# Twenty-six columns of an input projection by Strassen's seven products, ahead of a paged decode

## Chip, cores and metric

One NeuronCore of a Trainium2 chip runs the whole kernel. The metric is the device time of one execution in microseconds, lower is better. The kernel before has a median of 1408.3 us over three runs (1408.06 to 1410.06).

## What is computed

One layer of an inference step over 512 prompt tokens and 32 decode tokens (8 sequences of 4). Everything is float32.

```python
h = rmsnorm(x, norm_w)
p = jnp.einsum('btd,de->bte', h, w_in)          # 2048 x 8192
qa, ka, va, za, qb, fb, ib, zb = jnp.split(p, offs, axis=-1)   # 8 heads of 128 each
# group A: stick-breaking attention; the decode tokens also read 2048 past tokens from a paged cache
z = jnp.einsum('bqhd,bkhd->bhqk', q, k) * scale + bias
log_1m = jnp.where(causal, jax.nn.log_sigmoid(-z), 0.0)
tail = lax.cumsum(log_1m, axis=3, reverse=True) - log_1m
w = jnp.where(causal, jnp.exp(jax.nn.log_sigmoid(z) + tail), 0.0)
o_a = jnp.einsum('bhqk,bkhd->bqhd', w, v)
# group B: HGRN2 recurrence, exact per token, in chunks
S_t = diag(f_t) S_{t-1} + k_t v_t^T;  o_t = S_t^T q_t
m = concat(head_rmsnorm(o_a) * silu(za), head_rmsnorm(o_b) * silu(zb))
y = rmsnorm(x + m @ w_out, final_norm_w)
```

The keys, the values and the recurrent states of the new tokens are outputs too.

## The kernel before

The 544 tokens are kept normalised and transposed in SBUF as `h_hi` and `h_lo`, two float32r parts whose sum is the token value, in two halves of the 2048 inputs (`kh`). The input projection has 64 column tiles of 128 columns; `project` (L381) computes one of them in PSUM as 96 matmuls: two halves of the inputs, two halves of the tokens (256 and 288 of them, `HALVES`), eight slices of 128 inputs, and three part products each (weight hi by token hi, weight hi by token lo, weight lo by token hi). L408 scales the result on its way to SBUF. The weights come 512 KB at a time: `load_ahead` (L244) issues the transfer on SP's queue into `wraw` (three buffers), `split_ahead` (L252) makes `whi` on ACT (L259) and `wlo` on DVE (L260), and `weights_piece` (L268) keeps both ahead of the matmuls. The output projection (L1106) takes its weights in the same way.

The order on PE and SP is written by a small planner, `Flow`. It walks over the matmuls of the projection, and every two groups of four it may put in a piece of a side job. A side job is a generator that yields its cost, a time it should wait, and a gate: the share of the columns that must be done before. The other engines' instructions are put in an order that fits this one. The columns are taken in this order: the 8 q columns of group A, kept in DRAM (`q_dram`, L957); then in `group_a` (L927) k, v and z_a of each head, with its `attend` (L455) as a side job; then in `group_b` (L1007) q_b, f, i and z_b of each head, with its `hgrn` (L705). Next to both runs `decode` (L645): 32 key steps (L678) of 1/32 of the cached keys each, whose pages SP fetches (`k_fetch`, L540, 2 MB a step, three `kpage` buffers of 1 MB) and DVE transposes (L550), and 32 value steps (L688), 4 steps behind, on pages of `v_fetch` (L561, 2 MB a step, ten `vpage` buffers of 256 KB). The 36 steps are spread evenly by their gate between 1/8 and 0.87 of the columns:

```python
yield (32 * 56.0 if keys else 0.0) + (8 * 213.0 if values else 0.0), \
    (8000.0 if step == 0 else 3000.0), 0.0, start + (stop - start) * step / NSTEP
```

In `hgrn`, SP loads the head's old states into two `bst` tiles (L724), `usp` (L897) and L900 on DVE update them at the end of the head, and L902 on POOL stores them. A head is begun when the one before has issued these stores (`hg_done`). After the last column come the rest of the output projection and the final norm.

## Time and profile before

| | |
|---|---|
| median of three runs | 1408.3 us |
| the profiled execution, its own time | 1405.46 us |
| its span in the trace | 1403.8 us |
| PE busy | 1331.7 us (95%) |
| DVE, ACT, POOL busy | 758.3, 413.6, 311.7 us |
| projection matmuls (L401) | 6144 |
| HBM read and written | 239.15 and 19.53 MB |
| granted TensorE clock | 0.985 of full speed |

The profiled execution took 1.66 us more than its span, and the median lies 2.8 us above it. Busy times are averages over stages with different limits: the first columns run alone on PE, then the columns share it with decode, and behind them come the last columns and the output projection. Each stage has to be read for itself.

### The profile page before, as it was taken

The numbers are of one execution on the slowest core, as the hardware profiler recorded it, in microseconds if no ns is written. First come the engines' busy times: TensorE is split into PE (matmuls) and PEld (weight loads), VectorE is DVE, ScalarE is ACT, GpSimd is POOL, SyncE is SP. The second block draws the span as 40 slices with busy tenths as digits, with TensorE's granted clock in tenths as the row PEclk, the third lists the DMA queues.
The fourth block names the chain that finished last, engine by engine and source line by source line (L and its number), as shares of the span: only waits on it lengthen the run. The fifth ranks groups of instructions, "written<-read, shape, count | busy, mean of one in ns | idle before, by whom it ended". The sixth has DMA issues, their size and how long they took to land.

```text
span 1403.8 us, 30662 instructions
## 1 busy us (share of the span) xinstructions
PE 1331.7 (95%) x11922; PEld 1215.2 (87%) x11922; DVE 758.3 (54%) x1302; ACT 413.6 (29%) x701; POOL 311.7 (22%) x577
## 2 busy tenths in 40 slices
PE   6999999899999999999989989999999999999997
PEld 6999888798988888888887978889899897988996
DVE  6324555647466474667575674665455658222223
ACT  6211324224233242331222231132323225222223
POOL 3212113112132121132332232121213324111001
PEclk9999999999999999999999999999999999999999
DMA  7338876699989898898888978746523251622223
GB/s 218 109 109 214 200 203 163 174 292 235 280 228 269 236 258 220 229 273 212 247 231 233 274 193 235 229 143 196 149 61 113 65 194 42 240 76 78 89 76 143
DMA packets 245027, 260.69 MB, mean 186 GB/s; under 512 B 13497, under 2 KB 169842, under 8 KB 244178
## 3 DMA queue, kind: packets, MB, share of 16 engines
q1 hardware_dynamic: 237600, 235.00, 60.5%
q0 software_dynamic: 5504, 15.80, 3.3%
q10 hardware_dynamic: 1778, 7.93, 1.5%
q8 instruction: 94, 1.54, 0.5%
q14 instruction: 51, 0.42, 0.1%
HBM read 239.15 MB, written 19.53 MB: 184 GB/s over the span
## 4 chain that ended last, share of the span: by engine, by line
PE 74%; issue 10%; DVE 9%; DMA 3%; ACT 3%; POOL 1%; SPq 0%; DVEq 0%; POOLq 0%; ACTq 0%
PE pacc L401 42%; PE yacc L1106 13%; DVE kpage L550 3%; PE av L688 3%; PE dzp L678 3%; PE sp L746 2%; DMA kpage<-in_cache_k 2%; PE op L507 1%; PE usp L897 1%; PE ysp L1115 1%; DVE wlo L260 1%; DMA wraw<-in_w_in 1%; DVE lt L450 1%; DVE att L803 1%; PE wp L174 1%
## 5 line engine op out<-in xcount | busy, mean ns | idle before, releaser
L401 PE MATMUL pacc<-h_hi,whi 128*128 128x256 f32 (+1 forms) x2048 | 546.4, 299 | 15.2 <-ACT whi L259 9.8
L401 PE MATMUL pacc<-h_lo,whi 128*128 128x256 f32 (+1 forms) x2048 | 530.4, 289 | 0.0
L401 PEld LDWEIGHTS pacc<-h_hi,whi 128*128 128x128 f32 x2048 | 389.1, 190 | 40.1 <-issue 22.9
L401 PEld LDWEIGHTS pacc<-h_lo,whi 128*128 128x128 f32 x2048 | 389.2, 190 | 1.7 <-issue 0.2
L260 DVE TENSOR_TENSOR wlo<-wraw,whi 128x1024 fp32r<-128x1024 f32 x160 | 198.0, 1240 | 199.0 <-PE yacc L1106 78.0
L259 ACT CAST whi<-wraw 128x1024 fp32r<-128x1024 f32 x160 | 166.6, 1046 | 458.3 <-PE pacc L401 312.7
L401 PE MATMUL pacc<-h_hi,wlo 128*128 128x256 f32 (+1 forms) x2048 | 294.6, 292 | 0.0
L401 PEld LDWEIGHTS pacc<-h_hi,wlo 128*128 128x128 f32 x2048 | 269.5, 189 | 13.0 <-issue 12.3
L550 DVE STREAM_TRANSPOSE kpage<-kpage 128x2048 f32<-128x2048 f32 x64 | 146.2, 2296 | 0.2 <-issue 0.2
L1106 PE MATMUL yacc<-whi,m_hi 128*128 128x256 f32 x512 | 130.4, 293 | 0.0
L1106 PE MATMUL yacc<-whi,m_lo 128*128 128x256 f32 x512 | 126.7, 285 | 3.1 <-DVE m_lo L1096 3.0
L1106 PEld LDWEIGHTS yacc<-whi,m_hi 128*128 128x128 f32 x512 | 98.8, 193 | 16.8 <-issue 13.0
L1106 PEld LDWEIGHTS yacc<-whi,m_lo 128*128 128x128 f32 x512 | 99.1, 194 | 3.6 <-DVE m_lo L1096 3.5
L678 PE MATMUL dzp<-kpage,qblk 128*32 128x128 f32 x2048 | 68.3, 281 | 23.1 <-DVE kpage L550 23.0
L678 PEld LDWEIGHTS dzp<-kpage,qblk 128*32 128x32 f32 x2048 | 54.8, 112 | 33.0 <-DVE kpage L550 27.4
L1106 PE MATMUL yacc<-wlo,m_hi 128*128 128x256 f32 x512 | 68.3, 282 | 0.0
L1178 POOL TENSOR_TENSOR y<-y,fnw 128x512 f32<-128x512 f32 (+1 forms) x18 | 26.3, 1477 | 178.7 <-DVE y L1174 111.2
L1106 PEld LDWEIGHTS yacc<-wlo,m_hi 128*128 128x128 f32 x512 | 64.3, 191 | 0.0
L688 PE MATMUL av<-vpage,dwt 128*32 128x512 f32 x512 | 62.2, 600 | 0.0
L658 POOL COPY qblk<-q_new 32x32 f32<-32x32 f32 x128 | 45.7, 357 | 31.0 <-PE dzp L678 25.8
L746 PE MATMUL sp<-bE,kr 128*128 128x192 f32 x256 | 47.4, 326 | 1.9 <-DVE o_s L596 1.4
L803 DVE COPY_PREDICATED att<-lvls,sp 128x192 f32<-128x192 uint8 (+2 forms) x144 | 38.3, 310 | 15.9 <-PE sp L746 14.9
(262 smaller groups left out, 1372.3 us busy)
## 6 DMA issues: line engine op xcount, KB each, us to landing
wraw<-in_w_in SPq DMA_DIRECT2D x128, 512.0 KB, 5.9
kpage<-in_cache_k SPq DMA_DIRECT2D x256, 256.0 KB, 5.5
vpage<-in_cache_v SPq DMA_DIRECT2D x256, 256.0 KB, 5.1
wraw<-in_w_out SPq DMA_DIRECT2D x32, 512.0 KB, 3.5
bst<-in_state_s SPq DMA_DIRECT2D x16, 256.0 KB, 6.2
out<-bst POOLq DMA_DIRECT2D x16, 256.0 KB, 3.9
y<-in_x_prompt ACTq DMA_DIRECT2D x4, 1024.0 KB, 7.4
xt<-in_x_prompt SPq DMA_DIRECT2D x7, 512.0 KB, 5.8
```

The costliest lines, as they stand in the source:

```text
L174: nc.tensor.transpose(out, in_, ident[:k, :k])
L259: turns.append(nc.scalar.copy(hi, raws[i]))
L260: nc.vector.tensor_tensor(lo, raws[i], hi.bitcast(F32), ALU.subtract)
L401: nc.tensor.matmul(ps[half][:, :n], a[:, j, :], x[:, j, ts], start=(kh == 0 and part == 0 and r == 0), stop=(kh == 1 and part == 1 and r = ...
L550: nc.vector.transpose(flat, flat)
L658: nc.gpsimd.tensor_copy(out.rearrange("p h (g x) -> p h g x", g=4)[:, :, :, :DT], q_new[32 * j:32 * j + 32, :, DT * b:DT * b + DT].rearran ...
L678: nc.tensor.matmul(zp[32 * g:32 * g + 32, gp * P:(gp + 1) * P], qb[:, at:at + 32], kt[:, g, :, 32 * j:32 * j + 32], start=(gp == 0 and h2 ...
L688: nc.tensor.matmul(av[hf][32 * i:32 * i + 32, :], wt[:, gp, i, :], vpending[n], start=(gp == 0), stop=(gp == 3))
L746: nc.tensor.matmul(sp[:, i * 192:(i + 1) * 192], kr[:, n * P:(n + 1) * P], moving(n), start=True, stop=True)
L803: nc.vector.copy_predicated(a4[:, :, :, d * hl:], m.unsqueeze(1).to_broadcast([P, 2, u, w]), s4[:, :, :, at:at + w])
L1106: nc.tensor.matmul(out, m[4 * kq + j][:, c], b[:, j, :], start=(kq == 0 and part == 0 and r == 0 and (one or tb % 2 == 0)), stop=(kq == 3 ...
L1178: nc.gpsimd.tensor_tensor(part, part, fnw[:, cs].unsqueeze(1).to_broadcast([P, n, CG]), ALU.mult)
```

## The change

The columns are put in a new order, and 26 of them are computed in another way. First, alone on PE, come 4 q columns as before, and then 26 columns in 13 couples: the other 4 q, the 8 z_a, the 8 q_b and 6 of the z_b columns. A couple is a 2 x 2 block product (two columns, two halves of the inputs, two halves of 272 tokens), done with the seven products of Strassen's method in Winograd's form. Each product is 24 matmuls of 272 columns (`project_two`), so a couple takes 168 matmuls in place of 192, and the 13 couples 312 fewer. The block sums of tokens are made once, during the second and third column (`token_sums`); those of weights for every couple (`operand`: three on POOL, one on DVE). The products are summed in PSUM and, from copies that ACT makes, on DVE and POOL. All 30 results are stored to DRAM (`p_dram`) by POOL's queue and loaded again by SP's where a head needs them (`load_gate`, `load_query`, `ql`).

After that come the 34 columns that are left: k and v of each head, f and i of each head, and two z_b columns. The 36 steps of decode are spread over 0 to 0.87 of these. The planner's wait between the two transposes of a key step falls from 14000 to 9000, and a head of `hgrn` is begun when its predecessor's outputs are there (`hg_past`), before that one's state update and stores (`hg_done`). The tokens stand in another order in `h_hi` and `h_lo`, 256 prompt and 16 decode tokens in each half, and eviction follows it.

```diff
--- before.py
+++ after.py
+    PLAIN = 4
+    ZLATE = 2
+    ahead_cols = [h * P for h in range(PLAIN, H)] + [3 * W + h * P for h in range(H)] \
+        + [4 * W + h * P for h in range(H)] + [7 * W + h * P for h in range(H - ZLATE)]
+    couples = list(zip(ahead_cols[::2], ahead_cols[1::2]))
...
+    columns = [c for h in range(H) for c in (W + h * P, 2 * W + h * P)]
+    columns += [c for h in range(H) for c in (5 * W + h * P, 6 * W + h * P)]
+    columns += [7 * W + h * P for h in range(H - ZLATE, H)]
+    plan = [("in", kh, h * P) for h in range(PLAIN) for kh in range(2)]
+    plan += [("st", pair, k) for pair in couples for k in range(7)]
+    plan += [("in", kh, col) for col in columns for kh in range(2)]
...
+        if e[0] == "st":
+            (c1, c2), k = e[1:]
+            q = quads.setdefault(e[1], {})
+            if k == 0:
+                q["11"] = raw_tile(in_view(0, c1), wpool, "wraw", 3)
+            elif k == 1:
+                q["21"] = raw_tile(in_view(0, c2), sp_, "sraw", 3)
+                q["22"] = raw_tile(in_view(1, c2), wpool, "wraw", 3)
+            elif k == 3:
+                q["12"] = raw_tile(in_view(1, c1), sp_, "sraw", 3)
...
+        q, k = quads[plan[i][1]], plan[i][2]
+        if k == 1:
+            q["s"] = sp_.tile([P, 1024], F32, name="ssum", bufs=1)
+            nc.gpsimd.tensor_tensor(q["s"], q["21"], q["22"], ALU.add)
+        elif k == 2:
+            nc.gpsimd.tensor_tensor(q["21"], q["11"], q["21"], ALU.subtract)
+            nc.vector.tensor_tensor(q["s"], q["s"], q["11"], ALU.subtract)
+        elif k == 5:
+            nc.gpsimd.tensor_tensor(q["12"], q["12"], q["s"], ALU.subtract)
+        return q[("11", "s", "s", "12", "21", "12", "22")[k]]
...
+        def less(eng, a, b):
+            d, e = temp(), temp()
+            eng.tensor_tensor(d, a[0], b[0], ALU.subtract)
+            eng.tensor_tensor(e, a[1], b[1], ALU.subtract)
+            eng.tensor_tensor(d, d, e, ALU.add)
+            return d
...
+        def keep_sum(eng, i, x):
+            hi, lo = sums[i]
+            nc.scalar.copy(hi[:, j], x)
+            eng.tensor_tensor(lo[:, j], x, hi[:, j].bitcast(F32), ALU.subtract)
+
+        t1 = less(nc.vector, block(0, 1), block(0, 0))
+        keep_sum(nc.vector, 0, t1)
+        t2 = less_sum(nc.vector, block(1, 1), t1)
+        keep_sum(nc.vector, 1, t2)
+        keep_sum(nc.vector, 3, less_sum(nc.vector, block(1, 0), t2))
+        keep_sum(nc.gpsimd, 2, less(nc.gpsimd, block(1, 1), block(0, 1)))
...
+        def scaled(eng, out, th, x):
+            c = slice(256 * th, 256 * th + 256)
+            eng.tensor_tensor(out[:, c], x[:, NH * th:NH * th + 256], rbc[:, c], ALU.mult)
+            c = slice(SEQ + NH * th, SEQ + NH * th + NH)
+            eng.tensor_tensor(out[:, c], x[:, 256 * (1 - th):256 * (1 - th) + NH], rbc[:, c], ALU.mult)
...
+        def held(name, bank):
+            t = sp_.tile([P, XH], F32, name=name)
+            nc.scalar.copy(t, bank[:, :XH])
+            return t
+
+        def joined(out, th, bank, part):
+            t = sp_.tile([P, XH], F32, name="sj", bufs=2)
+            nc.vector.tensor_tensor(t, bank[:, :XH], part, ALU.add)
+            scaled(nc.gpsimd, out, th, t)
...
+        steps = [(a, plain(0, 0), True), (b, sums[0], True), (a, sums[1], False), (c, plain(1, 0), True),
+                 (a, sums[2], False), (b, plain(1, 1), False), (a, sums[3], False)]
...
+            todo = [(j, w, x[part]) for part, w in enumerate((hi, hi)) for j in range(8)]
+            todo = [todo[8 * part + j] for j in range(8) for part in range(2)] + [(j, lo, x[0]) for j in range(8)]
+            for r, (j, w, m) in enumerate(todo):
+                if r % STEP == 0:
+                    yield STEP * (XH / 2.4 + 2.0)
+                nc.tensor.matmul(bank[:, :XH], w[:, j, :], m[:, j, :], start=(fresh and r == 0), stop=(r == 23),
+                                 skip_group_check=True)
...
+    def load_gate(pool, hh, col):
+        zt = tp_.tile([P, T], F32, name="zt", tag="az")
+        nc.sync.dma_start(zt, p_dram[place[col]])
+        gate(hh, zt, pool.tile([P, T], F32, name="sgm", tag="sg"))
+        return zt
...
-                yield 0.0, (0.0 if step == 0 else 14000.0), 0.0, 0.0
+                yield 0.0, (0.0 if step == 0 else 9000.0), 0.0, 0.0
...
+    def load_query(h):
+        nc.sync.dma_start(kr[:, :T], p_dram[place[4 * W + h * P]])
+
+    def hgrn(h, F, it, res):
+        q = kr[:, :T]
...
+        if h < H - ZLATE:
+            res["zt"] = load_gate(bp_, H + h, 7 * W + h * P)
...
+        if h < H - 1:
+            load_query(h + 1)
...
+        hg_past[h] = True
...
+    def store_part(col, out):
+        nc.gpsimd.dma_start(p_dram[place[col]], out)
+        if col < W:
+            nc.gpsimd.tensor_copy(q_new[:, col // P, :], out[:, SEQ:])
...
+                if h in (1, 2) and i % 12 == 4:
+                    token_sums(2 * (h - 1) + i // 12)
...
+        for n, pair in enumerate(couples):
+            yield from project_two(pair, n, store_part)
...
-    flow.done, flow.total = 0, 64 * 24
+    flow.run(first_part(), per=2)
...
+    k_fetch(3)
+    flow.done, flow.total = 0, (4 * H + ZLATE) * 24
+    flow.add(decode(0.0, STOP), 2)
...
-                flow.wait(lambda: hg_done[h - 1])
...
+                flow.wait(lambda: hg_past[h - 1])
+            else:
+                open_b()
+                load_query(0)
+            flow.add(hgrn(h, F, it, ress[h]), 0)
```

POOL, in a couple of the first part (`ssum`, `sraw` are sums of weights, `so` the results, `sj` the joined products). Before, POOL had between two of the first columns only this:

```order
L956 COPY q_new<-qt 128x32
L957 DMA q_dram<-qt 128x512
L658 COPY qblk<-q_new 32x2x4x4 x16
L456 COPY k_new<-kt 128x32
```

and now has for each couple:

```order
L290 TENSOR_TENSOR sraw<-sraw,ssum 128x1024
L285 TENSOR_TENSOR ssum<-sraw,wraw 128x1024
L287 TENSOR_TENSOR sraw<-wraw,sraw 128x1024
L506 TENSOR_TENSOR so<-sj,rbc 128x256
L508 TENSOR_TENSOR so<-sj,rbc 128x16
L506 TENSOR_TENSOR so<-sj,rbc 128x256
L508 TENSOR_TENSOR so<-sj,rbc 128x16
L506 TENSOR_TENSOR so<-sj,rbc 128x256
L508 TENSOR_TENSOR so<-sj,rbc 128x16
L1080 DMA p_dram<-so 128x544 x2
```

Three sums of 128x1024 and six scalings have come in, all in one queue with the two stores.

SP, where the states of the second head of `hgrn` are loaded. Before:

```order
L249 DMA wraw<-in_w_in 128x8x128 x2
L724 DMA bst<-in_state_s 128x4x128 x2
L249 DMA wraw<-in_w_in 128x8x128
L540 ISA
L540 DMA kpage<-in_cache_k 32x4x512
```

and now (`kr` is the head's q from `p_dram`):

```order
L849 DMA kr<-p_dram 128x544
L254 DMA wraw<-in_w_in 128x8x128
L871 DMA bst<-in_state_s 128x4x128 x2
L254 DMA wraw<-in_w_in 128x8x128
L683 ISA
L683 DMA kpage<-in_cache_k 32x4x512
```

The state loads stand ahead of a key fetch in both; a load from `p_dram` has come in before them.

POOL, where the first head's states are stored (`out<-bst`). Before, both stores stand together, ahead of the next head's first product:

```order
L902 DMA out<-bst 128x4x128 x2
L720 TENSOR_TENSOR prod_9701<-bf 128x272
L784 COPY pre<-prod_9701 128x64
L785 COPY suf<-prod_9701 128x64
L786 TENSOR_TENSOR pre<-prod_9701 128x64
```

and now the next head's work lies between and after them:

```order
L1044 TENSOR_TENSOR bkn<-bvs,bmask 32x512
L1053 DMA out<-bst 128x4x128
L867 TENSOR_TENSOR prod_11851<-bf 128x272
L931 COPY pre<-prod_11851 128x64
L932 COPY suf<-prod_11851 128x64
L933 TENSOR_TENSOR pre<-prod_11851 128x64
L934 TENSOR_TENSOR suf<-prod_11851 128x64
L935 TENSOR_TENSOR pre<-pre,prod_11851 128x64
L936 TENSOR_TENSOR suf<-prod_11851,suf 128x64
L937 TENSOR_TENSOR prod_11852<-pre,suf 128x64
L1053 DMA out<-bst 128x4x128
```

The next head is begun before the stores of the one before it are issued, while its loads still go into the same two `bst` tiles.

## Rows read from the trace of the kernel before

**Rows 1.** The page: busy time and share of the span of each engine.
```profile
PE 1331.7 (95%) x11922; PEld 1215.2 (87%) x11922; DVE 758.3 (54%) x1302; ACT 413.6 (29%) x701; POOL 311.7 (22%) x577
```

**Rows 2.** Chain of waits, from the start to the end of decode: start us, us, what.
```profile
40.30 94.79 PE pacc L401 x752
135.09 1.88 PE dzp L678 x64
...
917.31 1.88 PE dzp L678 x64
...
1008.25 1.85 PE av L688 x16
```

**Rows 3.** Stretches: us from:to, length, busy of each engine (instructions), PEclk, DMA share, GB/s.
```profile
35.00:135.00 100.00, 99.80 (x790) 99.24 (x789) 35.58 (x47) 18.40 (x22) 20.11 (x37) 1.00 0.52 143
135.00:600.00 465.00, 435.32 (x4274) 397.03 (x4274) 271.13 (x379) 152.29 (x274) 91.98 (x178) 0.99 0.85 229
600.00:917.00 317.00, 299.27 (x2909) 267.48 (x2908) 204.24 (x393) 76.83 (x119) 81.29 (x183) 0.99 0.85 233
```

**Rows 4.** The same two long stretches, projection matmuls (L401) alone: PE, PEld, clock, DMA.
```profile
135.00:600.00 465.00, 325.38 (x2362) 306.11 (x2362) 0.99 0.85 229
600.00:917.00 317.00, 208.64 (x1517) 195.58 (x1516) 0.99 0.85 233
```

**Rows 5.** Short stretches: 100 us of decode, then keys alone, values alone, weights and stores.
```profile
280.00:380.00 100.00, 97.66 (x953) 88.99 (x952) 55.49 (x79) 32.62 (x57) 17.91 (x37) 0.98 1.00 268
491.00:497.00 6.00, 6.00 (x47) 5.76 (x47) 2.31 (x4) 1.05 (x1) 0.00 (x0) 1.00 1.06 231
499.00:502.00 3.00, 3.00 (x27) 2.98 (x26) 2.27 (x5) 2.79 (x6) 1.29 (x4) 1.00 1.03 374
503.00:508.00 5.00, 5.00 (x42) 5.00 (x42) 4.95 (x11) 3.11 (x7) 1.62 (x4) 1.00 1.05 325
```

**Rows 6.** The page: GB/s in 40 equal slices of the span (35.1 us each).
```profile
GB/s 218 109 109 214 200 203 163 174 292 235 280 228 269 236 258 220 229 273 212 247 231 233 274 193 235 229 143 196 149 61 113 65 194 42 240 76 78 89 76 143
```

**Rows 7.** PE's longest wait: who waited for what, us in total, times, longest.
```profile
PE dzp L678 <- DVE kpage L550: 23.0, 15, 3.4
```

**Rows 8.** Waits of SP's queue: the state loads.
```profile
SPq L724 <- DMA out<-bst: 12.7, 3, 4.8
```

**Rows 9.** DMA issues: line, queue, count, KB each, median us to landing.
```profile
kpage<-in_cache_k SPq DMA_DIRECT2D x256, 256.0 KB, 5.5
...
out<-bst POOLq DMA_DIRECT2D x16, 256.0 KB, 3.9
```

**Rows 10.** Groups by line and shape: busy us, mean ns of one, idle before.
```profile
L260 DVE TENSOR_TENSOR wlo<-wraw,whi 128x1024 fp32r<-128x1024 f32 x160 | 198.0, 1240 | 199.0 <-PE yacc L1106 78.0
L259 ACT CAST whi<-wraw 128x1024 fp32r<-128x1024 f32 x160 | 166.6, 1046 | 458.3 <-PE pacc L401 312.7
...
L711 DVE TENSOR_TENSOR bE<-bq,sgm 128x544 f32<-128x544 f32 x8 | 5.9, 735 | 1.5 <-ACT sgm L219 1.4
```

**Rows 11.** The same for POOL.
```profile
L902 POOL DMA_DIRECT2D out<-bst x16 | 12.5, 778 | 40.7 <-DVE bst L900 38.8 <-DMA wraw<-in_w_out 1.9
...
L355 POOL TENSOR_TENSOR h_lo<-xtmp,h_hi 128x512 fp32r<-128x512 f32 x8 | 11.2, 1397 | 17.8 <-ACT h_hi L353 17.7
L418 POOL TENSOR_TENSOR sq<-ot 128x512 f32<-128x512 f32 x8 | 8.3, 1040 | 100.7 <-DVE ot L510 100.6
```

**Rows 12.** Timeline of POOL, 1180 to 1196 us: start, us, instruction, idle before.
```profile
1183.10 1.28 POOL L1096 TENSOR_TENSOR m_lo<-vpage,m_hi 128x512 fp32r<-128x512 f32 x1
...
1188.18 2.17 POOL L1096 TENSOR_TENSOR m_lo<-vpage,m_hi 128x512 fp32r<-128x512 f32 x1 [1.53 <-ACT m_hi L1094]
```

**Rows 13.** Timeline of DVE in the same stretch.
```profile
1180.15 0.68 DVE L1096 TENSOR_TENSOR m_lo<-kpage,m_hi 128x512 fp32r<-128x512 f32 x1
...
1187.98 1.23 DVE L260 TENSOR_TENSOR wlo<-wraw,whi 128x1024 fp32r<-128x1024 f32 x1 [0.18 <-issue]
1189.12 1.78 DVE L1096 TENSOR_TENSOR m_lo<-vpage,m_hi 128x512 fp32r<-128x512 f32 x1
```

194 lines of the change are left out of this document (115 added, 79 removed).

## The prediction

> **What bounds the kernel now.** I read the busy shares first: PE works 95% of the span [rows 1]. That average hides three stages, so the chain of waits comes next. From 40 to 135 us it is one piece of projection, 752 matmuls in 94.79 us [rows 2]: 0.126 us each, 12.1 us for a column of 96, nothing beside it. The first key step follows at 135.09, the 32nd and last at 917.31, the last value step ends at 1010 [rows 2]: 31 key intervals of 25.2 us. The stretches show what fills them. PE is busy 435.32 of 465 and 299.27 of 317 us, and the DMA engines carry a share of 0.85 in both [rows 3]. So decode's 782 us leave PE 47 us and DMA about 117 us of slack: PE is the bound, DMA close behind. The 100 us from 280, with a share of 1.00 at 268 GB/s [rows 5], show both full at once. The rest, from 917.31 to 1403.8, is PE again.
>
> **Work removed.** 13 couples save 24 matmuls each: 312 by 0.126, 39.2 us of PE. If nothing else changed, the span would be 1364.6. Everything below asks what of it survives, since the change also squeezes decode into fewer columns.
>
> **First part, start to first key step.** Before it took 135.1 us with 8.75 columns ahead. Four columns instead of eight, and 0.75 before the step: 135.1 less 4.75 by 12.1 gives 77.6. Couples add 13 x 168 x 0.126 = 275.2, the 0.75 column 9.1: 361.9. Three terms come on top.
> - The page buffers are opened only after the first part, so the first page must land (5.5 us [rows 9]) and be transposed. 9.1 us of matmuls cover most of that: +4 (0 to 10).
> - Token sums: four calls of ten DVE and four POOL operations on 544 elements. At 0.735 us [rows 10] that is 29 us of DVE, and for POOL 16 x 1.0 to 1.4 [rows 11], 16 to 22. Splits and evictions of the three columns add some 10 to DVE, in about 37 us before the first sum is wanted: +5 (0 to 20).
> - Each couple costs DVE 8 operations of 1.24 (7 splits, one sum) and under 2 us of joins, ACT 7 x 1.05 and three copies [rows 10], POOL three sums of twice L418's size (2.1 to 2.8 each), six scalings worth 1.5 to 2.1 in all and two store issues of 0.78 [rows 11]: 12, 9 and 9.5 to 12 us, beside 21.2 of PE. Engine by engine this fits.
>
> But DVE and POOL don't always work side by side. At 1187.98 a DVE split of 1.23 us starts; POOL's L1096 starts at 1188.18 and needs 2.17, where one needed 1.28 [rows 12]; DVE's next, from 1189.12, needs 1.78 where one needed 0.68 [rows 13]. Each lasted as if it had waited for the other. The narrow place is the third product, whose weights need DVE's subtraction behind the second's split, and then ACT's copy. From the end of the product before the couple (3.0 us each), when a weight buffer comes free, that is 1.05 + 1.24 + 1.24 + 1.05 = 4.6 of 6.0 us; one POOL sum of 2.5 in DVE's way makes it 7.1 and misses by 1.1: 0 to 15 over 13 couples. Most splits keep to a mean of 1.24 [rows 10], so I take +4. The Trainium skill (SBUF — State Buffer, Who interferes with whom) says that a DVE instruction with two inputs in SBUF contends with a GpSimd one that reads SBUF, and that the loser is blocked. These rows agree; by that rule alone the sums on POOL would cost the upper end, 15.
>
> First key step at 361.9 + 13 = 375.
>
> **Key steps, first to last.** In the order of the change 27.2 columns stand between them, before it was 40.4: 16.6 in the 17 intervals beside the attends (0.98 each), 10.6 in the 14 beside `hgrn` (0.76). Side work I take from the long stretches: 435.32 less 2362 x 0.126 and some 19 key and 15 value steps of 1.9 leaves 74 us for eight attends, 9.3 each; 299.27 likewise leaves 63 for about four heads of `hgrn`, 16 each [rows 2 to 4]. Per interval:
> - Attends: PE 11.8 + 3.7 + 0.49 x 9.3 = 20.1. DMA: 2.1 MB of keys at 231 GB/s is 9.1, of values at 374 is 5.6, 1.02 MB of weights and 0.63 of head traffic at 325 is 5.1 [rows 5]: 19.8.
> - `hgrn`: PE 9.2 + 3.7 + 6.0 = 18.9. DMA: 9.1 + 5.6 + 1.5 MB at 325 (4.6) = 19.3.
>
> The first four intervals have no values, 18.3 each. 4 x 18.3 + 13 x 20.1 + 14 x 19.3 = 605. DMA and PE now weigh the same, and two bounds stand beside this. PE can't go under its busy time of before, 734.6, less 13.2 columns (160) plus one more head (16): 590. DMA moved 106 + 74 = 180 MB there [rows 3]; less 13.9 of weights, plus about 6 of reloaded parts and one head's states, it moves 172: 643 us at 268 GB/s [rows 5], 590 at the best slice's 292 [rows 6].
>
> Then waits. Key steps waited 23.0 us for transposes [rows 7]; with less slack I keep +10. And the state loads: they wait for the old head's stores, on the queue that fetches keys. They did so three times, 12.7 us in all [rows 8]; now the next head starts before those stores. At two of four heads within the key steps both `usp` follow the key fetch by up to 0.37 column, 4.5 us, then side work, DVE's update, a store issue of 0.78 [rows 11] and 3.9 to land [rows 9]: some 16 us for which SP holds back keys. Of these 10 to 16 are lost, since transfers issued earlier run on; at the other two 0 to 4. That is 20 to 40; I take 23. Sum 605 + 10 + 23 = 638 (590 to 683), where before it was 782.
>
> **Last key step to the end.** 486.5 before. 8.8 fewer columns remain (106.5), one `hgrn` fewer (16). The last four value steps now lie within 0.54 column instead of 4: fetching 8.4 MB at 374 takes 22 us, PE has about 9 meanwhile: +13 (0 to 20). 377.
>
> **Sum:** 375 + 638 + 377 = 1390 span, against 1403.8. The profiled run was 1.66 longer than its span, the median 2.8 above that: **1394**.
>
> **Rivals.**
> - *A, transfers keep up.* If DMA reaches the 292 GB/s of a whole slice, the key steps go at PE's pace: 590 over before's PE share of 0.94 is 627, first part 368, end 370: 1365, so 1370. For it: 1.00 share beside 97.66 us of PE in 100 [rows 5], and a shorter wait between transposes. Against: no value-carrying average but one above 280 [rows 6].
> - *B, the fetch queue decides.* Transfers stay at 268 GB/s (643) and the state loads block SP for the full 40 us. Then 375 + 683 + 377 = 1435: 1439, slower. It decides once the key steps take over 652, a rate below 265 without any blocking, or 275 with 27 lost. For it: stores in the way already at three heads [rows 8]. Against: with three page buffers a short delay drains only part of a step.
> - *C, the first part stalls.* The exclusive use of rows 12 and 13 costs the 15 us in the couples, the token sums 20, the page load 10: 32 more than my 13, so 1426, and down to 1414 where the token sums alone are late by less. If DVE and POOL excluded each other entirely, a couple would need up to 9.9 + 12 us against 21.2, so it can't grow much beyond.
> - *D, the saving is not there* because 272-column products take longer than the mean 272 of halves: excluded, the streamed columns are the same; at most what PE gains is hidden, which B covers.
>
> **Chances.** Forecast 0.46, with its own range of 1380 to 1408; A 0.26, B 0.18, C 0.10. The measurement can tell 0.2%, 2.8 us. A and 0.33 of the forecast's 0.46 lie below 1405.5, plus 0.01 of C: faster 0.60. Around 1408: 0.09 (0.07 of the forecast, the weak edge of B and C). Slower 0.31, B and C nearly whole and the forecast's upper tail. The range goes from 1362, a little under A, to 1434, short of B's full price: it leaves out A's lower tail and half of B.
>
> **What would show it.** Right: the first key step near 375; couples in one unbroken piece of the chain, 21.2 us each; key steps 19 to 20 us apart beside attends, DMA share 0.93 or more between the first and the last; SP waits of L871 for the stores of over 10 us at two heads, with PE waiting for the transposes right after; the last value steps waiting for `vpage`. Wrong: key intervals under 19 with DMA share below 0.9 (A); L871's waits small and the intervals still over 21 (transfers alone); gaps of PE at the third product of a couple (C); L871's waits over 30 in sum with a last key step after 1025 (B).

## The result, and the profile after

The changed kernel takes 1559.25 us (median of four runs, 1553.53 to 1565.11), the kernel before in the same comparison 1409.18. The ratio is 1.1057, with an interval of 1.1006 to 1.1107: 10.6% slower, where 1% faster was forecast, and well outside the range that was given. The profiled execution took 1558.53 us with a span of 1556.6.

The page of the changed kernel, busy time of each engine, answers to [rows 1]:

```profile
PE 1361.9 (87%) x11610; PEld 1209.1 (78%) x11610; DVE 900.4 (58%) x1445; ACT 477.1 (31%) x795; POOL 512.6 (33%) x733
```

PE has 312 instructions fewer and is idle for 195 us instead of 72. Where, the stretches tell, with the columns of [rows 3]: token sums, couples, key steps beside the attends, key steps beside `hgrn`, and what follows.

```profile
35.00:107.50 72.50, 48.59 (x344) 47.60 (x343) 59.32 (x68) 18.77 (x27) 35.48 (x24) 0.81 0.27 77
107.50:381.00 273.50, 273.50 (x2183) 273.50 (x2182) 175.15 (x169) 106.38 (x130) 187.50 (x145) 1.00 0.41 121
397.00:793.00 396.00, 335.39 (x3235) 289.21 (x3224) 236.35 (x347) 127.78 (x239) 80.47 (x168) 0.91 0.87 238
793.00:1159.00 366.00, 300.30 (x2770) 246.43 (x2768) 225.26 (x460) 84.53 (x140) 98.50 (x227) 0.92 0.82 220
1159.00:1330.00 171.00, 150.72 (x1065) 125.77 (x1064) 99.67 (x258) 49.45 (x80) 52.58 (x102) 0.93 0.45 138
```

The couples are perfect: PE is busy for all of 273.5 us, 21.04 us a couple. Before them PE is idle for 24 us. In the key steps PE is busy for 85% and 82% of the time (94% before) and DMA for a share of 0.87 and 0.82. Neither is full. The forecast had taken one of them to be full at any time.

The first, the 18th and the last key step in PE's timeline (start, us, instruction, idle before) bound the stages:

```profile
396.57 1.94 PE L821 MATMUL dzp<-kpage,qblk 128*32 128x128 f32 x32 [6.16 <-DVE kpage L693]
...
793.18 1.08 PE L821 MATMUL dzp<-kpage,qblk 128*32 128x128 f32 x32
...
1159.04 1.08 PE L821 MATMUL dzp<-kpage,qblk 128*32 128x128 f32 x32
```

| stage | before | forecast | measured | off by |
|---|---|---|---|---|
| start to first key step | 135.1 | 375 | 396.6 | +21.6 |
| 17 key intervals beside the attends | | 340 | 396.6 | +57 |
| 14 key intervals beside `hgrn` | | 298 | 365.9 | +68 |
| both | 782.2 | 638 | 762.5 | +124 |
| last key step to the end | 486.5 | 377 | 397.5 | +21 |
| span | 1403.8 | 1390 | 1556.6 | +167 |

(The forecast's 638 is divided here by its own terms: 334 and 270 us, the transposes' 10 divided about evenly, the 23 of the state loads to `hgrn`.) Three quarters of the miss lie among the key steps. They show in two ways. PE is idle there for 126 us, and it is busy for 636 (335.39 and 300.30 above), where the forecast had put its work at 590. The longer busy time is in the matmuls of decode itself. On the page they had 68.3 us (key steps) and 62.2 (value steps) before; now:

```profile
L821 PE MATMUL dzp<-kpage,qblk 128*32 128x128 f32 x2048 | 83.1, 314 | 89.3 <-DVE kpage L693 89.3
L831 PE MATMUL av<-vpage,dwt 128*32 128x512 f32 x512 | 94.0, 713 | 3.4 <-DMA vpage<-in_cache_v 3.4
```

That is 46.6 us more for the same matmuls, at a granted clock of 0.91 and 0.92 instead of 0.99. PE's waits, answering to [rows 7]:

```profile
PE dzp L821 <- DVE kpage L693: 89.3, 29, 7.0
PE pacc L444 <- DVE so L451: 23.7, 2, 12.8
PE sp L570 <- POOL sqlo L566: 22.1, 6, 6.0
PE sp L893 <- DVE kr L864: 12.5, 4, 4.2
PE sp L893 <- issue: 10.1, 1, 10.1
```

The transposes of key pages stand first, with 89.3 us against 23.0. SP's queue, answering to [rows 8]:

```profile
SPq L871 <- DMA out<-bst: 159.8, 14, 22.4
SPq L683 <- PE dzp L821: 136.6, 34, 15.4
```

The state loads wait 159.8 us for stores instead of 12.7. That makes three candidates: state loads block the fetch queue (Q), transfers are too slow (T), or the order on DVE is wrong for the new spacing (O). A fourth one, too few page buffers, was not tried. One step tells a good deal already. Here are the timelines of PE, SP and DVE around the key step at 544 us; L693 is the transpose of a page, two in a row on DVE being the second half of one step and the first of the next:

```profile
518.63 1.94 PE L821 MATMUL dzp<-kpage,qblk 128*32 128x128 f32 x32 [1.65 <-DVE kpage L693]
537.94 1.08 PE L821 MATMUL dzp<-kpage,qblk 128*32 128x128 f32 x32
544.13 1.93 PE L821 MATMUL dzp<-kpage,qblk 128*32 128x128 f32 x32 [5.11 <-DVE kpage L693]
```
```profile
518.12 6.13 SPq L683 DMA_DIRECT2D kpage<-in_cache_k  x6
```
```profile
516.27 4.50 DVE L693 STREAM_TRANSPOSE kpage<-kpage 128x2048 f32<-128x2048 f32 x2
527.26 0.42 DVE L453 TENSOR_TENSOR vt<-pacc,rbc 128x256 f32<-128x256 f32 x1 [6.50 <-PE pacc L444]
...
530.13 1.28 DVE L608 TENSOR_SCALAR z<-zp,sbb 128x512 f32<-128x512 f32 x2
...
534.03 2.07 DVE L594 TENSOR_TENSOR_SCAN lt<-ones_r,lt 128x512 f32<-128x512 f32 x2
...
540.64 1.22 DVE L302 TENSOR_TENSOR wlo<-wraw,whi 128x1024 fp32r<-128x1024 f32 x1
541.77 4.50 DVE L693 STREAM_TRANSPOSE kpage<-kpage 128x2048 f32<-128x2048 f32 x2
```

The old step ends at 520.6. The page that the next step's second half needs has landed at 524.3, as its semaphore shows. DVE transposes it at 541.8 only. In between it waits 6.5 us for PE, to evict a column, and then works off a chain of `attend` that stands ahead of the transpose in its queue. PE has begun the step at 537.9 and stands for 5.1 us before its second half.

Over all 17 intervals beside the attends (worked out from the records of each step): the page lands 3.8 us after the step before, its transpose begins at 19.4, and in 29 of 31 steps the second half of the key step starts within 0.5 us of its end. In the kernel before, the second transpose begins 20.2 us after the step before and ends at 22.5 (mean of all 31 intervals; 20.3 and 22.6 in the changed kernel). There steps were 25.2 us apart, and the waits came to 23.0 us. The delay is the same in both kernels. The forecast wanted steps 19 to 20 us apart.

### The profile page after: what moved, and what is told of

It is laid out like the page before. It is cut to its first block, busy times and chain, and to the rows that moved or that the text cites. A ratio compares the mean times of both kernels' runs of the same rounds, so it can differ in the third digit from the quotient of the medians.

```text
span 1556.6 us, 30648 instructions
## 1 busy us (share of the span) xinstructions
PE 1361.9 (87%) x11610; PEld 1209.1 (78%) x11610; DVE 900.4 (58%) x1445; ACT 477.1 (31%) x795; POOL 512.6 (33%) x733
## 4 chain that ended last, share of the span: by engine, by line
PE 61%; DVE 10%; issue 9%; DMA 9%; ACT 4%; POOL 2%; SPq 1%; POOLq 0%; DVEq 0%; ACTq 0%
PE pacc L444 16%; PE yacc L1264 12%; PE pa L529 10%; PE pb L529 5%; PE av L831 4%; DVE kpage L693 4%; DMA vpage<-in_cache_v 3%; PE pc L529 3%; PE dzp L821 2%; DMA kpage<-in_cache_k 2%; PE sp L893 2%; PE ysp L1273 1%; DVE lt L594 1%; DVE wlo L302 1%; PE op L652 1%
## 5 line engine op out<-in xcount | busy, mean ns | idle before, releaser
L444 PE MATMUL pacc<-h_hi,whi 128*128 128x288 f32 (+1 forms) x1216 | 345.9, 313 | 28.0 <-DVE so L451 23.7
L444 PE MATMUL pacc<-h_lo,whi 128*128 128x288 f32 (+1 forms) x1216 | 327.4, 297 | 0.0
L301 ACT CAST whi<-wraw 128x1024 fp32r<-128x1024 f32 x134 | 140.2, 1047 | 472.0 <-PE pacc L444 231.8
L444 PEld LDWEIGHTS pacc<-h_hi,whi 128*128 128x128 f32 x1216 | 241.1, 198 | 53.3 <-issue 45.9
L444 PEld LDWEIGHTS pacc<-h_lo,whi 128*128 128x128 f32 x1216 | 240.8, 198 | 1.8 <-issue 0.5
L444 PE MATMUL pacc<-h_hi,wlo 128*128 128x288 f32 (+1 forms) x1216 | 183.1, 298 | 0.0
L444 PEld LDWEIGHTS pacc<-h_hi,wlo 128*128 128x128 f32 x1216 | 164.9, 193 | 12.4 <-issue 11.7
L821 PE MATMUL dzp<-kpage,qblk 128*32 128x128 f32 x2048 | 83.1, 314 | 89.3 <-DVE kpage L693 89.3
L693 DVE STREAM_TRANSPOSE kpage<-kpage 128x2048 f32<-128x2048 f32 x64 | 146.1, 2297 | 17.6 <-DMA kpage<-in_cache_k 17.6
L831 PE MATMUL av<-vpage,dwt 128*32 128x512 f32 x512 | 94.0, 713 | 3.4 <-DMA vpage<-in_cache_v 3.4
L302 DVE TENSOR_TENSOR wlo<-sraw,whi 128x1024 fp32r<-128x1024 f32 x39 | 62.2, 1595 | 33.7 <-ACT whi L301 33.7
L893 PE MATMUL sp<-bE,kr 128*128 128x192 f32 x256 | 53.9, 355 | 22.6 <-DVE kr L864 12.5
L1264 PE MATMUL yacc<-wlo,m_hi 128*128 128x256 f32 x512 | 68.3, 282 | 0.0
L893 PEld LDWEIGHTS sp<-bE,kr 128*128 128x128 f32 x256 | 45.5, 206 | 26.0 <-issue 16.2
```

What stands on the lines that cost most here:

```text
L301: turns.append(nc.scalar.copy(hi, raw))
L302: nc.vector.tensor_tensor(lo, raw, hi.bitcast(F32), ALU.subtract)
L444: nc.tensor.matmul(ps[half][:, :n], a[:, j, :], x[:, j, ts], start=(kh == 0 and part == 0 and r == 0), stop=(kh == 1 and part == 1 and r = ...
L693: nc.vector.transpose(flat, flat)
L821: nc.tensor.matmul(zp[32 * g:32 * g + 32, gp * P:(gp + 1) * P], qb[:, at:at + 32], kt[:, g, :, 32 * j:32 * j + 32], start=(gp == 0 and h2 ...
L831: nc.tensor.matmul(av[hf][32 * i:32 * i + 32, :], wt[:, gp, i, :], vpending[n], start=(gp == 0), stop=(gp == 3))
```

## Experiments

All times beside the changed kernel's 1559.25 us; an interval is of the ratio to the kernel before.

**Undo the earlier start of `hgrn`'s heads.**

```diff
-                flow.wait(lambda: hg_past[h - 1])
+                flow.wait(lambda: hg_done[h - 1])
```

> The changed kernel with one line undone: a head of hgrn begins only when the head before has issued its state stores. Theory Q (SP's queue is held up by state loads that wait for stores: 160 us of such waits in all, 80 of them among the key steps): those waits fall under 30 us, the key steps from the 18th to the last, 366 us in the changed kernel, take 310 or less, the time falls to about 1500. Theory O (the key steps stand so close in the order that DVE cannot have the second page of a step transposed in time, so PE and DVE wait for each other in turn): those waits go too, but the time stays above 1535, and PE's waits for transposes stay above 70 us (89 in the changed kernel). Theory T (transfers are simply too slow): the same as O for the time.

1543.98 us (1.0935 to 1.1006), 15 less. SP's waits for state stores fall from 159.8 to 64.8 us, those among the key steps from 79.6 to 23.1, and the 14 intervals from 366 to 333 us. PE's waits for transposes stay at 87.5. So blocking is part of the loss beside `hgrn`, but as a whole worth a tenth of the loss: Q is not the main cause. (The steps stand closer in this order, too: 1.8 columns have moved behind them, and 18 of the 33 us come back there.)

**Squeeze decode in the kernel before, nothing else.**

```diff
-        flow.add(decode(H / 64, STOP), 2)
+        flow.add(decode(28 / 64, STOP), 2)
...
-                yield 0.0, (0.0 if step == 0 else 14000.0), 0.0, 0.0
+                yield 0.0, (0.0 if step == 0 else 9000.0), 0.0, 0.0
```

> The kernel before, with nothing of the products, the new column order or the reloads; only decode starts at 28 of 64 columns instead of 8, and the planner's wait between the two transposes is 9000 as in the change. Key steps then stand 0.93 columns apart in the order, as in the change. Theories O and T: the squeeze is the cause, so this kernel is slower too: key steps 24 us apart or more, PE waits for transposes over 70 us (23 before), time 1480 or more. Theory Q, or the reloads as the cause: key steps about 20 us apart and a time under 1430.

1455.33 us (1.0305 to 1.0376): 48 us slower than before, between the two expectations. The second half of a step now waits for its transpose in 30 of 31 steps, 63.6 us in all, and intervals are 21.6 us, with the second transpose ending 20.1 us after the step before. Squeezing alone costs nearly a third of what the change lost. In this kernel the squeezed stretch holds one or two attends and six heads of `hgrn`; in the changed one, with two columns a head left instead of four, eight attends and five heads.

**Halve the value transfers; transposes earlier in the planner's time.**

```diff
+            if len(vpending) % 2:
+                vpending.append(vpending[-1])
+                continue
             t = dp.tile([P, 512], F32, name="vpage", bufs=NV)
```

> The changed kernel, but only every second value page is fetched and used twice, so half of the cached values are left out: 32 MB fewer, about 1 MB for each key interval. Theory T: at 270 GB/s the intervals shorten by 3.5 us each, the time falls by 80 us or more, to 1480 or less. Theory O: DMA was idle a sixth of the time anyway, the time falls by less than 30 us. Theory Q: the same as O.

1536.57 us (1.0886 to 1.0949). 32 MB fewer bring 23 us, not 80; DMA's share in the stretch to 830 us falls to 0.78. T is out as the first limit.

```diff
-                yield 0.0, (0.0 if step == 0 else 9000.0), 0.0, 0.0
+                yield 0.0, (0.0 if step == 0 else 5000.0), 0.0, 0.0
```

> The changed kernel with the planner's wait between the two transposes of a key step 5000 instead of 9000, so that the second transpose stands earlier in DVE's order, and the key steps 0.80 columns apart instead of 0.88. Theory O: the second transposes no longer queue behind the chains of attend, but the steps stand still closer; intervals stay 23 to 26 us, the waits of PE for transposes 80 us or more, DVE now waits for the pages to land (over 40 us, 18 in the changed kernel). The time lies between 1530 and 1590. Theory T: unchanged within 15 us.

1553.24 us (1.1004 to 1.1068), 6 less, and 80.2 us of waits for transposes. Beside the attends the second transpose comes at 16.7 us instead of 19.4 and the 17 intervals take 21.1 us, less than the 23 to 26 expected. But only 13.2 columns lie among these steps now, by the records of the matmuls, where it was 15.8:

```profile
398.00:756.00 358.00, 297.26 (x2924) 252.68 (x2920) 207.42 (x298) 106.88 (x201) 66.91 (x148) 0.91 0.94 252
```

PE is idle for 61 us there, as before. The key stretch gets 57 us shorter, and 51 of them come back behind it: projection has moved, the waits have not gone. An interval says something only beside the columns in it.

**Spread the token sums; undo the products.**

```diff
-                if h in (1, 2) and i % 12 == 4:
-                    token_sums(2 * (h - 1) + i // 12)
+                if (h, i) in ((1, 4), (1, 20), (2, 12), (3, 4)):
+                    token_sums(((1, 4), (1, 20), (2, 12), (3, 4)).index((h, i)))
```

> The changed kernel, with the four calls that make the token sums spread over columns two to four instead of two and three. If the 30 us by which the first couple starts late come from PE standing behind evictions that DVE does after the sums (waits for so, 23.7 us), these waits fall under 8 us and the couples start at 90 or before instead of 107.5; the time falls by 15 to 25 us. If the sums are simply too much work for DVE and POOL, the couples start as late as before.

1558.43 us (1.0998 to 1.114), not the 15 to 25 us less that were expected. The waits only move: 12.8 us at one eviction, 7.6 at another. The first couple starts at 102, not at 90 or before, and the first key step comes at 393.3.

```diff
-    plan += [("st", pair, k) for pair in couples for k in range(7)]
+    plan += [("in", kh, col) for pair in couples for col in pair for kh in range(2)]
...
-            yield from project_two(pair, n, store_part)
+            for col in pair:
+                out = sp_.tile([P, T], F32, name="so", bufs=4)
+                yield from project(out, col)
+                store_part(col, out)
```

> The changed kernel with the products undone: the same 26 columns come first in the same order and go to DRAM in the same way, but each is computed plainly with 96 matmuls; there are no sums. All theories that put the loss into the stage after the first part: the stretch from the first to the last key step stays within 15 us of 762, the first part gets 312 x 0.126 = 39 us longer and loses the 30 us of the token sums, the time is 1555 to 1580. If the products themselves hurt what follows, it would be under 1530.

1567.32 us (1.1073 to 1.1191). The first key step comes at 407.1, and from the first to the last it is 766 us, as in the changed kernel. Two things follow. The products do no harm behind the first part; what has changed beside them (the order of the columns, the squeezed decode, the reloads, the early heads) loses the time. And they are worth 10.5 us at the first key step, not 39: the token sums take the rest.

**Take the transposes away; take the key transfers away.**

```diff
-            flat = t.rearrange("p s e -> p (s e)")
-            nc.vector.transpose(flat, flat)
```

> The changed kernel without the 64 transposes of key pages on DVE, which leaves this part of the computation out; everything else stands in the same order and the pages are fetched as before. Theory O (the transposes stand too late in DVE's queue): the key steps no longer wait for DVE, PE's waits at the key steps fall from 89 to under 30 us and the key stretch from 762 to 690 or less. Theory T or Q (the pages come late): PE waits for the pages themselves, 60 us or more, and the stretch stays above 725.

1473.58 us (1.0417 to 1.0515), 86 less, and the key stretch is 686 us. PE waits 14.7 us for pages. The stretch of its 17 intervals beside the attends:

```profile
397.00:736.00 339.00, 324.20 (x3228) 284.47 (x3232) 162.17 (x313) 128.56 (x242) 83.37 (x169) 0.98 1.03 274
```

20.1 us an interval, at a DMA share of 1.03 and 274 GB/s. That is close to the 19.8 us and the full DMA of the forecast, reached once no transposes stand between. This is the cleanest test of the record: the order on PE is the same, with 15.8 columns in the 17 intervals as in the changed kernel, and 54 of the 57 us lost there are gone. The 14 intervals beside `hgrn` lose 22 of their 68. It does not tell a transpose that stands late from one that takes DVE's time; for that see the forced order below.

```diff
+            if len(kpending) >= 3:
+                kpending.append(kpending[-3])
+                continue
             t = dp.tile([P, 4, 512], F32, name="kpage", bufs=3)
```

> The changed kernel, fetching only the first three key pages and using them over and over, with all transposes and matmuls kept: 61 of the 64 MB of keys are left out. Theory T or Q: key intervals lose most of their waits, the key stretch falls from 762 to 660 or less. Theory O: the transposes stand in the same places of DVE's queue, PE waits for them as long as before (70 us or more) and the stretch stays above 715.

1406.44 us (0.9968 to 1.0028), 153 less, which is what T and Q had said of it. It does not speak for them all the same. DVE's order is made from an estimate of when pages come, and without transfers it puts the transposes elsewhere: the second one begins 0.3 us after the step before, not 20.3, and is ready 16 us before it is used.

```profile
PE pacc L444 <- DVE so L451: 23.7, 2, 12.8
PE sp L896 <- DVE kr L867: 12.5, 4, 5.9
PE dzp L824 <- DVE kpage L696: 10.4, 2, 5.7
```
```profile
397.00:1017.00 620.00, 589.40 (x6035) 518.45 (x6039) 455.40 (x810) 212.00 (x381) 170.84 (x396) 0.98 0.58 179
```

The wait at the key steps is 10.4 us and PE is busy for 95%. So this run removes transfers and late transposes at once, and cannot tell them apart by its time. It does show two things. With nearly all waits of the key steps gone, the stretch is 621 us and the whole no faster than the kernel before. And PE's busy time for the same matmuls falls to 589.40 us, the forecast's 590, at a granted clock of 0.98:

```profile
L824 PE MATMUL dzp<-kpage,qblk 128*32 128x128 f32 x2048 | 64.5, 279 | 10.4 <-DVE kpage L696 10.4
L834 PE MATMUL av<-vpage,dwt 128*32 128x512 f32 x512 | 71.7, 594 | 1.1 <-DMA vpage<-in_cache_v 1.0
```

So the slower clock of the changed kernel came with its waits.

**Keep all transfers and force the transposes ahead on DVE.** `issue_after` puts DVE's instructions of a side job behind the last transpose, while the attends run.

```diff
-        req = next(s[1], None)
+        with (self.tc.issue_after(self.turn.ins) if self.turn is not None else ExitStack()):
+            req = next(s[1], None)
...
-            nc.vector.transpose(flat, flat)
+            turn = nc.vector.transpose(flat, flat)
+            flow.tc, flow.turn = tc, None if bp_ else turn
...
-                yield 0.0, (0.0 if step == 0 else 9000.0), 0.0, 0.0
+                yield 0.0, (0.0 if step == 0 else 4000.0), 0.0, 0.0
```

> The changed kernel, while the attends run, with the second transpose of a key step forced ahead in DVE's order: the planner's wait before it is 4000, and whatever the side jobs give DVE after it is put behind it. Pages, transfers and PE's order rules stay. Theory O (a page lies landed for some 15 us because its transpose stands behind a chain of attend in DVE's order): the second transposes come 6 to 12 us after the step before instead of 19, PE's waits at the key steps of this part fall to under 20 us, the 17 intervals from 23.3 to 20 or 21 us each, the time falls by 30 to 60 us from 1559. Theory T: DVE now waits for the pages instead, the intervals stay at 23.

1529.01 us (1.0815 to 1.0911), 30 less. The second transpose begins at 12.9 us instead of 19.4, and PE waits 42.0 us at the key steps instead of 89.3. The 17 intervals take 20.3 us each instead of 23.3:

```profile
397.00:742.00 345.00, 296.79 (x2924) 252.61 (x2924) 205.91 (x299) 106.09 (x201) 65.61 (x148) 0.93 0.97 257
```

The interval alone overstates it: 13.2 columns lie in these 17 intervals, as in the run with 5000, and of 76 us that the key stretch loses, 51 come back after it. Beside that run, with the same columns among these steps, the intervals fall from 21.1 to 20.3 us, PE's waits for transposes there from 45.1 to 21.0, and the time by 24 us. The same pages, the same queue, another order on one engine: this is O, and it separates it from T. The share of DMA is now 0.97, and DVE waits 21.3 us for pages there. Transfers are the second limit, right behind the first, near the price the forecast gave.

```diff
-                (8000.0 if step == 0 else 3000.0), 0.0, start + (stop - start) * step / NSTEP
+                (8000.0 if step == 0 else 6000.0), 0.0, start + (stop - start) * step / NSTEP
```

> The changed kernel with the key step itself put 6000 of the planner's time behind its second transpose instead of 3000: key steps 1.05 columns apart in PE's order instead of 0.88, the last at the end of the columns. Theory O: PE now has projection to do where it stood waiting; waits at the key steps fall from 89 to under 45 us, the intervals stay 23 to 25 us, and since five columns less remain behind them the time falls by 35 to 70 us. Theory T: intervals grow only if the pages don't bound them; they stay as they are, and the time falls by as much.

1542.77 us (1.093 to 1.0991), 16 less, not 35 to 70. The waits for transposes fall to 35.2 us, yet the intervals grow to 27.6. Five columns more lie among the key steps, and PE is idle for 125 us among them as before: other waits have grown, for `kr` from 12.5 to 31.0 us and for `sqlo` from 22.1 to 33.2.

```diff
-    STOP = 0.87
+    STOP = 0.97
...
-                flow.wait(lambda: hg_past[h - 1])
+                flow.wait(lambda: hg_done[h - 1])
```

These two, together with the forced transposes:

> The forced order of the run before last, a head of hgrn only after the state stores of the one before, and the key steps spread to 0.97 of the columns instead of 0.87 (0.92 columns apart). All theories: better than any of these alone; theory O: 1460 to 1500, key intervals about 21. It stays slower than the kernel before, since the first part alone starts the key steps 20 us later than I had reckoned, and the heads of hgrn still stall.

1514.93 us (1.0729 to 1.0797), short of the 1460 to 1500 expected, and with intervals of 23.8 us instead of 21, but the fastest version of the changed kernel that computes everything.

**The planner's wait in the kernel before; the forced order in the kernel before.**

```diff
-                yield 0.0, (0.0 if step == 0 else 14000.0), 0.0, 0.0
+                yield 0.0, (0.0 if step == 0 else 9000.0), 0.0, 0.0
```

> The kernel before with one part of the change alone: the planner's wait between the two transposes of a key step 9000 instead of 14000; key steps stand at the same columns. PE waited 23 us for transposes there. Theory O: the second transposes come a few us sooner, the waits fall by 5 to 15 us, the time by 0 to 12 us. Theory T: no difference.

1401.3 us (0.9933 to 0.9968): faster than the kernel before, by 0.5%. But not as O expects, for the waits for transposes stay at 23.6 us in its profile. What gains is open; the profiled execution itself took 1407.29 us.

And the edit that forces the transposes, as above, with this line instead:

```diff
-                yield 0.0, (0.0 if step == 0 else 14000.0), 0.0, 0.0
+                yield 0.0, (0.0 if step == 0 else 6000.0), 0.0, 0.0
```

> The kernel before with the second transpose forced ahead in DVE's order while the attends run, and the planner's wait before it 6000 instead of 14000; nothing else of the change. Theory O: PE's waits at the key steps of that part (23 us in all before) fall by 8 to 15 us, the time by 4 to 15 us, below the kernel before and at or below the run with 9000. If PE's order fills these gaps anyway, no difference from that run.

1418.51 us (1.0058 to 1.0132), 0.95% slower. The waits for transposes do fall, from 23.0 to 17.3, but ten microseconds of new waits on ACT come at one place (`detp`) and nine at another (`dwtp`). Here the early transposes put off the chains behind them. The expectation fails.

**Beside `hgrn`: no state loads, and both cures.**

```diff
-            st = bp_.tile([P, 4, P], F32, name="bst", bufs=2)
-            nc.sync.dma_start(st, state_s[0, 4 * hf:4 * hf + 4, h].rearrange("b k v -> k b v"))
+            if h == 0:
+                st = bp_.tile([P, 4, P], F32, name="bst", bufs=2)
+                nc.sync.dma_start(st, state_s[0, 4 * hf:4 * hf + 4, h].rearrange("b k v -> k b v"))
+                held_states.append(st)
+            st = held_states[hf]
```

> The changed kernel, loading old states for the first head of hgrn only; the later heads go on with the same two tiles, so their old states are left out. Stores stay. SP's queue never waits for them. Theory Q2 (in the part beside hgrn, the queue held up by state loads is the main loss): the 14 intervals fall from 26.1 to 22 or less, the time by 50 us or more. Theory O2 (the transposes again, and the chains of hgrn): the intervals fall by 1 to 2.5 us each, the time by 15 to 40.

1530.23 us (1.0849 to 1.0893), 29 less; the 14 intervals take 25.0 us instead of 26.1. That is O2's range: with the queue never blocked, the steps stay late.

The same, with the forced transposes and 4000, and no end to the forcing where `hgrn` begins:

```diff
-            nc.vector.transpose(flat, flat)
+            flow.tc, flow.turn = tc, nc.vector.transpose(flat, flat)
```

> The run without the later state loads, and the second transpose forced ahead in DVE's order throughout (wait 4000), beside hgrn too. If the two causes make up the loss among the key steps, the 17 intervals take 20 to 21 us and the 14 take 20 to 22, the key stretch falls from 762 to 660 or less and the time to 1470 or less. If it stays above 1500, something else holds the steps back there, the chains of attend and hgrn that wait for each other on DVE.

1528.27 us (1.0826 to 1.0888): 31 less, where the two cures alone had brought 30 and 29. They don't add up. Beside the attends it is 19.8 us an interval, with 13.2 columns in them; beside `hgrn` 25.0, no better than without the forced order:

```profile
397.00:742.00 345.00, 297.48 (x2996) 252.74 (x3000) 212.90 (x304) 106.23 (x201) 65.01 (x148) 0.94 0.98 263
742.00:1087.00 345.00, 288.27 (x2709) 246.88 (x2705) 216.47 (x427) 91.36 (x158) 87.32 (x210) 0.91 0.83 229
```

Transposes are early there too (13.8 us) and the pages unblocked, yet neither PE nor DMA is full. PE now waits for the chains of `hgrn` (`sp` for `kr`, `bE`, `sgm`, some 40 us), and SP stands 43.6 us at L851, the new load of a head's q into `kr`, until DVE has done with the old one. The expectation that the two causes make up the loss fails beside `hgrn`, and for the time as a whole.

**All token sums on DVE.**

```diff
-        keep_sum(nc.gpsimd, 2, less(nc.gpsimd, block(1, 1), block(0, 1)))
+        keep_sum(nc.vector, 2, less(nc.vector, block(1, 1), block(0, 1)))
```

> The changed kernel with the POOL part of the token sums (16 of 56 operations) on DVE. If DVE and POOL shut each other out while both read two operands from SBUF, DVE's 56 operations take 0.72 us each, about 41 us in all, as long as its 40 took beside POOL (44 us), and the couples start within 4 us of 107.5. If DVE is just overloaded, they start 10 to 14 us later.

1551.95 us (1.0999 to 1.1051). With 16 operations more on DVE the couples start at 102.4, 5 us sooner than in the changed kernel; in the eleven runs whose first part is that of the changed kernel they start between 104.2 and 108.6. PE's wait at the two evictions is still 20.3 us. From the groups of DVE between 35 us and the couples, the same lines in the changed kernel and, second, in this run:

```profile
L478 DVE TENSOR_TENSOR so<-h_hi,so 128x544 f32<-128x544 f32 x8 | 9.1, 1136 | 0.4
L485 DVE TENSOR_TENSOR sum1lo<-so,sum1hi 128x544 fp32r<-128x544 f32 x4 | 8.4, 2107 | 0.0
```
```profile
L478 DVE TENSOR_TENSOR so<-h_hi,so 128x544 f32<-128x544 f32 x8 | 5.8, 721 | 0.2
L485 DVE TENSOR_TENSOR sum1lo<-so,sum1hi 128x544 fp32r<-128x544 f32 x4 | 2.9, 718 | 0.0
```

POOL's help cost 2 to 6 us more than it gave.

## Why the prediction was wrong, step by step

**First part: mis-sized by 22 us.** The couples came out as worked out, 273.5 us against 274 to 275, with no stall; the +4 for the third product and rival C's 15 there are 0. The term that failed is the token sums, put at +5: the forecast let DVE's work for them overlap with PE's three columns. In DVE's queue the evictions of two columns stood behind the sums, and PE waited 23.7 us for them, most of the 24 it was idle. The operations were also priced with durations of instructions that ran alone. Beside POOL, DVE's 40 operations took 1.10 us each on average, 43.9 in all, and POOL's 16 took 1.7. One pair of rows shows how (DVE, then POOL):

```profile
87.44 2.83 DVE L485 TENSOR_TENSOR sum1lo<-so,sum1hi 128x544 fp32r<-128x544 f32 x1
```
```profile
86.79 2.90 POOL L285 TENSOR_TENSOR ssum<-sraw,wraw 128x1024 f32<-128x1024 f32 x1 [5.89 <-DMA wraw<-in_w_in]
```

DVE's operation, 0.72 us alone, lasts until POOL's ends and 0.6 longer. The first couple started at 107.3, against 78.7 for the same place in the run with plain columns and no sums: 29 us for them, beyond even the upper bound of 20. The hindrance is the smaller part of it, since with all sums on DVE the couples still start at 102.4. The rule that the prediction weighed (the Trainium skill, SBUF — State Buffer, Who interferes with whom), that a DVE instruction with two inputs in SBUF contends with a GpSimd one that reads SBUF, agrees with these rows. The 15 us that were to follow from it in the couples did not come: the same hindrance is there, with DVE's splits of `sraw` and `wraw` at 1.60 and 1.76 us instead of 1.24, and PE had enough in hand to cover it.

**Key steps beside the attends: the wrong kind of sum, 57 us.** "PE 20.1, DMA 19.8" priced an interval as the larger of two engines' loads. Both prices were good as loads: without transposes DMA was full at 20.1 us an interval, without fetches PE was at 95%. What the sum left out is that a step is also a loop: free a page, fetch it, transpose it, use it. Each round of it took 22 to 23 us in the kernel before, with the page lying landed for 14 of them. In that loop stands DVE, at 54% busy never a suspect, in whose order the transpose stood behind chains that wait for PE. I took +10 for the 23.0 us of waits in [rows 7]; 89.3 came. The 23.0 were the sign that the loop was already nearly as long as the interval. PE's own term failed with it: 3.7 us for the key and the value matmuls of a step (4.1 by the page before) are 5.5 here (83.1 and 94.0 us over 32 steps), at the lower clock that came with the waits. Over all 31 intervals, PE's busy time is 46 us above the 590 of the forecast, and its idle time makes up the other 78 of the 124. A reading was off as well: by the records of the matmuls 15.8 and 11.4 columns lie in the 17 and the 14 intervals, not 16.6 and 10.6, which moves some 10 us of the miss from the second group to the first.

**Key steps beside `hgrn`: 68 us.** The state loads did block the queue, at about the price given (23 forecast; removing the loads gained 16 us in the 14 intervals). The rest is put down to the loop again (22 us less without transposes), and to the chains of `hgrn`, which with two columns a head instead of four stand closer together; that second part is argued and not shown. How the two divide stays open: with early transposes and unblocked pages the intervals stay at 25.0 us. The load of q into `kr`, which came into SP's order with the change and which the prediction did not price, is one of the new waits.

**The end: 21 us.** The forecast put +13 on the last four value steps waiting for their pages. They do come late: the first of them starts 34.5 us after the value step before it, and the last ends 64 us after the last key step, with 1.3 columns between in PE's order. But PE waited only 3.0 us for `vpage`, and more for the sum of squares of a finished head and for `kr`:

```profile
PE sp L570 <- POOL sqlo L566: 6.0, 1, 6.0
PE sp L893 <- DVE kr L864: 4.2, 1, 4.2
PE av L831 <- DMA vpage<-in_cache_v: 3.0, 2, 2.1
```

PE is idle for 18 us from the last key step to the last column, where it was 3 in the kernel before; in size that is the forecast's 13 and 2 more. The other 18 of the miss are PE's busy time: 149 us to the last column, where 253 before, less the forecast's 106.5 and 16, leave 131. The granted clock was 0.93 there; the cause was not tested.

**Rivals.** B named the right sign, but not the main mechanism, and its 1439 was far too small. Both of B's marks came (L871's waits over 30 us, a last key step after 1025), and taking the state loads away still gave back only 29 us: the marks did not tell B from O. D's reason was rightly put aside, at 21.04 us a couple, but its question, whether the saving is there, had another answer: 312 matmuls are gone, and 10.5 us are left of their 39 once the sums are paid.

**The range** missed because every case in it was a load of full engines with small waits on top. The intervals that the kernel before showed, 25.2 us with nothing full beside PE, would have been the case to include: 31 x 24.6 is what came out.

## What to carry to other kernels

Before work is packed closer, look for the loop that each step goes through, and read its length from the trace, not from the load of the engines on it: here it was 22.5 us from the end of a step to the end of the next second transpose, before and after the change. It was clearly shorter only where DVE's order or the spacing of the steps was changed (20.1 us in the squeezed kernel before, 17.8 with the forced transposes). A page that lies landed for 15 us points at the order on an engine that is half idle. When an interval gets shorter, count the columns in it before calling it a gain. And a saving on one engine that is paid with operations on DVE and POOL at once has to be priced with both slowed down, and with the evictions that stand behind them.

## What the runs showed of the hardware

DVE and POOL hindered each other where both read two operands from SBUF: DVE alone did a sum of 128x544 elements in 0.72 us (in the run with all sums on DVE, all groups but one lie between 0.714 and 0.722), beside POOL the lines shown above averaged 1.14 and 2.11 us. DVE's joins in the couples, with one operand from PSUM, were not slowed: 36 of the 39 ran beside an operation of POOL and took 0.44 us, as the other three did.

PE's granted clock fell with the gaps. It was 1.00 in the couples without a break, 0.81 in the 72 us of the token sums, and 0.91 and 0.92 in the key stretches, where before it was 0.99. After the wait of 12.75 us before 67.74, matmuls of 256 columns start 0.213 us apart, the lower of the two levels (1.2 GHz); from 71.3 on those of 288 start 0.131 us apart, the higher (2.4 GHz). What it cost among the key steps can be read from the same matmuls in two runs: PE was busy for 635.7 us with them in the changed kernel, and for 589.4 without key fetches, at 0.98. 41 of the 46 us are in the matmuls of decode, which come right behind the waits (177.1 us on the page against 136.2). By the clock's own records the lower level was granted for 129 us among the key steps of the changed kernel, and for 27 in the other run. So the clock followed the waits and added more than a third to what they cost.
